# A two-layer decoder trunk on one core: the block gather between two engines' layouts done as 16 SBUF copies instead of a trip through DRAM

## The chip, the cores and the metric

The kernel runs on one core of one Trainium2 chip. Its time is the device time of one launch in microseconds (us); less is better. The engines named here: PE (TensorE, matrix products and transposes), ACT (ScalarE), DVE (VectorE), POOL (GpSimd) and SP (SyncE, which only issues transfers here). Each engine works through its own instruction list in order, and instructions wait for one another by semaphores. SBUF is the on-chip memory with 128 partitions, PSUM the accumulators that PE writes, DRAM the large memory outside the core.

## The reference

A trunk of two layers on 256 positions of width 2048, all in float32. Cut to what is computed:

```python
for l in range(2):
    h = rms_norm(x, mix_norm[l])
    q, k, v, uv, gate_logits = split(h @ w_in[l])                  # 2048 x 7680
    q = rope(rms_norm(q, q_norm[l])); k = rope(rms_norm(k, k_norm[l]))
    a = sliding_window_attention(q, k, v, sinks[l]) @ w_attn_branch[l]   # 16 heads of 64, 4 kv heads
    b = chunked_sgu(gelu(uv), w_spatial[l], ...) @ w_sgu_branch[l]
    g = sigmoid(gate_logits)
    x = x + (g[:, :2048] * a + g[:, 2048:] * b) @ w_out[l]
    h2 = rms_norm(x, ffn_norm[l])
    x = x + (silu(h2 @ w_gate[l]) * (h2 @ w_up[l])) @ w_down[l]    # inner width 5632
```

## The kernel before, in words

**The products.** Every large product is a weight matrix (read once from DRAM) times activations of 256 positions. A float32 product is made of three reduced-precision ones: weights and activations are both split into a high part (`whi`, `uh`) and the rest (`wlo`, `ul`), and PE adds whi x uh, wlo x uh and whi x ul (lines 287 to 289). For that, a piece of weights of 256 x 512 arrives in `raw`, ACT copies it to `whi` (line 201), and DVE subtracts to get `wlo` (line 202). `raw` has 5 buffers and `whi` and `wlo` have 4 each, so the `whi` of one piece can't be written before PE is done with the piece four earlier.

**The stream.** All pieces of both layers stand in one list of 1010 entries, in PE's order (class `Stream`). At each entry the program asks for the raw piece 7 ahead (W_LOAD), the split 4 ahead (W_SPLIT) and sums of weights 6 ahead (W_SUM). A plain entry (X, G or U) has 12 matmuls of 128 x 512. The pairs of products `mix` (w_out), `ffn` (gate and up) and `hid` (down) use the Strassen-Winograd scheme for their first unit of activations: its entries P1 to P7 have 6 matmuls each, need sums of weights (line 189, DVE) and sums of activations (line 439, DVE, then split into `sh` and `sl` at lines 430 and 431), and copies of intermediate results, `snap` (line 313, ACT). The entries P1, P2, P6, P7 and P4 of a pair are woven between the last four entries of the plan before it; P6 accumulates on P1's result and so waits for P1's snap. The feed-forward part is done in three rounds per layer, of 4, 4 and 3 pairs `ffn`, each followed by two pairs `hid`.

**Activations as PE needs them.** PE wants the activations with the contracted dimension across partitions, so each 256 x 512 block of x, q, k, gate, hid and so on is transposed into a unit. Mostly that is done by `turn`: DVE transposes 32 x 32 blocks into `box` (line 355), and then the blocks have to move across partitions, the gather (lines 359 to 363). Before the change SP writes the box to a DRAM tile `far` (512 KB) and reads it back in four transfers into `tt` (128 KB each). ACT and DVE then scale and split `tt` into `uh` and `ul` (lines 381 to 390), or for Winograd units into `flat`, sums, `sh` and `sl`. For a few last units that are needed at once, PE transposes instead (`pt`, line 399).

**What sets the order.** PE's order is the program's own. The program counts ticks: one for about 12 matmuls of the stream; `after(n, f)` calls `f` n ticks later, and that is where turns, readers of turns and norms are put. The order of the other engines' lists is then made by a scheduler from a model of the timeline, with the ticks as the earliest place. `box` has one buffer.

Of the kernel before, what the change touches and what calls it, by code (L numbers as in the profile page):

```python
# [8 lines left out]
F32 = mybir.dt.float32  # L9
# [5 lines left out]
P = 128  # L15
NT = 2
# [17 lines left out]
WINO = 0  # L34
TAIL = 2
W_SPLIT = 4
W_SUM = 6
N_WARM = 8
TT = 1
# [12 lines left out]
def hybrid_trunk(ctx: ExitStack, tc: tile.TileContext, x, mix_norm, w_in, q_norm, k_norm, sinks,  # L52
# [9 lines left out]
    tmp = ctx.enter_context(tc.tile_pool(name="tmp", bufs=5))  # L62
    dram = ctx.enter_context(tc.tile_pool(name="dram", bufs=2, space=bass.MemoryType.DRAM))
    turned = ctx.enter_context(tc.tile_pool(name="turned", bufs=TT))
# [53 lines left out]

    def pair(key, wa, wb, late=False):
# [15 lines left out]
        body = [g[0], p5, g[1], p3] + g[2:-2] + u[:-TAIL] + g[-2:] + u[-TAIL:] if late else \  # L135
            [g[0], p5, g[1], p3] + g[2:] + u
        return Plan(key, head, body)

    plans = []
    for l in range(DEPTH):  # L140
        wl = w_in[l]
        for kind, c in FIRST_PART:
            o = {"kv": O_KV, "q": 0, "v": O_V, "u": O_U, "gate": O_GATE}[kind] + c * CW
            plans.append(single(("in", l), wl[:, o:o + CW]))
        plans += [single(("att", l), w) for w in cols_of(w_attn_branch[l], NCH)]
        for j in range(NCH):
            plans.append(single(("in", l), wl[:, O_GATE + D + j * CW:O_GATE + D + (j + 1) * CW]))
            plans.append(single(("sgu", l), w_sgu_branch[l, :, j * CW:(j + 1) * CW]))
        c_ = cols_of(w_out[l], NCH)
        plans += [pair(("mix", l), c_[j], c_[j + 1]) for j in range(0, NCH, 2)]  # L150
        for r, (f0, f1) in enumerate(ROUNDS):
            for f in range(f0, f1):
                plans.append(pair(("ffn", l), w_gate[l, :, f * CW:(f + 1) * CW], w_up[l, :, f * CW:(f + 1) * CW]))
            c_ = cols_of(w_down[l, f0 * CW:f1 * CW, :], NCH)
            plans += [pair(("hid", l, r), c_[j], c_[j + 1], j == 0) for j in range(0, NCH, 2)]
# [8 lines left out]
    class Stream:  # L164
# [41 lines left out]
        def next(self):  # L206
            self.load(self.at + W_LOAD)
            self.split(self.at + W_SPLIT)
            self.add(self.at + W_SUM)
            self.at += 1  # L210
            return self.parts[self.at - 1]
# [136 lines left out]
    def turn(dst, src):  # L348
# [7 lines left out]

        far = dram.tile([P, 4, 4 * NT * B], F32, tag="far", name=nm("far"))

        def gather():
            nc.sync.dma_start(far, box.rearrange("p j k t r -> p j (k t r)"))  # L360
            for j in range(4):
                nc.sync.dma_start(dst[j * B:(j + 1) * B].rearrange("c i k t r -> c i (k t r)"),
                                  far[:, j].rearrange("(i c) x -> c i x", c=B))

# [3 lines left out]
    def transposed(units, c, src, cols=None, on_pe=False, wino=False):  # L368
# [41 lines left out]
        if not wino:  # L410
# [3 lines left out]

            after(5, lambda: parts(0, 2, blocks_of(0)))
            after(6, done)
            return
# [28 lines left out]

        after(5, lambda: scaled(0))
        after(6, lambda: scaled(2))
        after(7, sums)
        after(8, finished)  # L450

# [36 lines left out]
    norm.unit(0, True)  # L488
    stream.split(W_SPLIT)
    after(1, lambda: norm.unit(1, True))  # L490
# [107 lines left out]
    class Attention:  # L598
# [65 lines left out]
        def turn_queries(self, c, q):  # L664
# [6 lines left out]
            turn(tt, q)  # L671
            after(4, lambda: ordered(0))
            after(5, lambda: ordered(2))

# [129 lines left out]
    def residual(key, nxt=None, scale=1.0, store=False):  # L804

        def chunk(j, sums):
# [11 lines left out]
            if nxt is not None:  # L818
                after(2, lambda: nxt.unit(j, j == NCH - 1))
                after(3, lambda: nxt.squares(j))  # L820
# [9 lines left out]
    for l in range(DEPTH):  # L830
# [31 lines left out]
        for j in range(NCH):  # L862
            gb = gate(l)
            ps = product(("sgu", l))
            for t in range(NT):
                nc.vector.scalar_tensor_tensor(out=gb[:, t, :], in0=gb[:, t, :], scalar=1.0, in1=ps[t],
                                               op0=ALU.add, op1=ALU.mult)
                nc.vector.tensor_tensor(out=ga[j][:, t, :], in0=ga[j][:, t, :], in1=gb[:, t, :], op=ALU.add)
            after(2, lambda j=j: transposed(mT, j, ga[j], on_pe=j == NCH - 1, wino=j == WINO))
            tick()  # L870
# [7 lines left out]
        def hidden(hT, c):  # L878
# [15 lines left out]
            def on_up(sums):  # L894
                up = added(sums)
                for t in range(NT):
                    nc.vector.scalar_tensor_tensor(out=hid[:, t, :], in0=up[t], scalar=norm.rr[t], in1=hid[:, t, :],  # L897
                                                   op0=ALU.mult, op1=ALU.mult)
                after(2, lambda: transposed(hT, c, hid, on_pe=c == len(hT) - 1 == 2, wino=c == WINO))

# [51 lines left out]
```

## Time and profile before

| | us |
|---|---|
| time, median of 3 runs (lowest to highest) | 2535.17 (2532.13 to 2540.45) |
| the profiled execution: its own time | 2530.42 |
| its span, first to last instruction | 2528.7 |
| PE busy | 2480.7 (98%) |
| DVE busy | 1906.9 (75%) |
| ACT busy | 1334.7 (53%) |
| POOL busy | 43.8 (2%) |

The mean granted clock of PE was 0.994 of full speed. The page has, per group of instructions, the line, the engine, the operation and the tiles (out<-in), then the busy time, the mean time of one in ns, and the engine's idle time just before them with what ended most of it. The view of waits lists, for one engine, who it waited for: the total in us, the number of times and the longest. The timeline has the start and the length in us; in brackets stands the idle time before and its releaser. Rows of stretches (A:B) list the length and, for PE, weight load, DVE, ACT and POOL, the busy time, then the granted clock, the share of the DMA engines and GB/s. An engine name with q is its queue of transfers.

### The profile page before, as it was taken

What the parts mean: (1) busy time and instruction counts of PE and PEld (TensorE: products, weight loads), DVE (VectorE), ACT (ScalarE), POOL (GpSimd) and SP (SyncE); (2) the same over time, 40 slices, a digit from 0 to 9 for tenths busy, and PEclk for the clock granted to TensorE, in tenths of its full rate; (3) what the DMA queues carried; (4) which work ended last, traced back from release to release, by engine and by line L of the source; (5) the groups of instructions that cost most, each with busy time, mean ns of one, the idle gap of its engine ahead of it and who ended that gap; (6) DMA issues with size and microseconds to landing.
All of it is one profiled execution on the core that took longest, in us unless ns stands there. A gap on an engine that the chain in (4) does not pass through costs nothing.

```text
span 2528.7 us, 30348 instructions
## 1 busy us (share of the span) xinstructions
PE 2480.7 (98%) x11094; PEld 2043.9 (81%) x11094; DVE 1906.9 (75%) x2293; ACT 1334.7 (53%) x1658; POOL 43.8 (2%) x47
## 2 busy tenths in 40 slices
PE   8999999999999999999999999999999999999999
PEld 7888888878788878887778888887778888788877
DVE  6786556787878787868877865568888777877787
ACT  5555444565555555555555554446555555555554
POOL 1100000000000000000000000000000000000000
PEclk9999999999999999999999999999999999999999
DMA  8755667676666667665776556666756666676654
GB/s 274 249 157 174 218 214 229 201 237 198 208 233 202 214 203 230 203 214 189 226 238 221 178 172 208 225 214 201 233 186 219 218 216 193 213 236 199 218 188 146
DMA packets 284823, 530.77 MB, mean 210 GB/s; under 512 B 18880, under 2 KB 46624, under 8 KB 284672
## 3 DMA queue, kind: packets, MB, share of 16 engines
q1 hardware_dynamic: 284000, 528.29, 64.5%
q8 instruction: 87, 1.43, 0.2%
q0 software_dynamic: 352, 0.25, 0.1%
q14 instruction: 64, 0.52, 0.1%
q10 hardware_dynamic: 320, 0.27, 0.0%
HBM read 500.96 MB, written 27.79 MB: 209 GB/s over the span
## 4 chain that ended last, share of the span: by engine, by line
PE 91%; DVE 3%; DMA 3%; ACT 2%; issue 1%; SPq 0%; DVEq 0%; ACTq 0%
PE acc L287 29%; PE acc L289 29%; PE acc L288 29%; DVE wlo L202 2%; ACT whi L201 1%; PE po L723 1%; DMA far<-box 1%; DMA raw<-in_w_in_dram 1%; PE psc L684 1%; PE ppt L713 0%; DMA raw<-in_w_gate_dram 0%; DVE raw L189 0%; DMA tt<-far 0%; PE pt L399 0%; DVE xs L813 0%
## 5 line engine op out<-in xcount | busy, mean ns | idle before, releaser
L202 DVE TENSOR_TENSOR wlo<-raw,whi 128x1024 fp32r<-128x1024 f32 (+1 forms) x1012 | 1227.7, 1220 | 506.9 <-ACT whi L201 487.6
L201 ACT ACTIVATE whi<-raw 128x1024 fp32r<-128x1024 f32 (+1 forms) x1012 | 1059.9, 1056 | 924.2 <-PE acc L289 682.6
L287 PE MATMUL acc<-whi,uh 128*128 128x512 f32 x3204 | 1257.2, 392 | 0.8 <-ACT uh L385 0.5
L289 PE MATMUL acc<-whi,ul 128*128 128x512 f32 x3204 | 1250.1, 390 | 3.9 <-DVE ul L390 3.9
L288 PE MATMUL acc<-wlo,uh 128*128 128x512 f32 x3204 | 1251.1, 390 | 2.7 <-DVE wlo L202 2.7
L289 PEld LDWEIGHTS acc<-whi,ul 128*128 128x128 f32 x3204 | 603.6, 188 | 131.4 <-DVE ul L390 4.8
L288 PEld LDWEIGHTS acc<-wlo,uh 128*128 128x128 f32 x3204 | 603.8, 188 | 130.6 <-DVE wlo L202 6.2
L287 PEld LDWEIGHTS acc<-whi,uh 128*128 128x128 f32 x3204 | 603.7, 188 | 127.4 <-ACT snap L313 1.5
L189 DVE TENSOR_TENSOR raw<-raw,raw 128x1024 f32<-128x1024 f32 x152 | 185.5, 1220 | 1.0
L287 PE MATMUL acc<-whi,sh 128*128 128x512 f32 x304 | 121.2, 399 | 26.4 <-ACT snap L313 26.4
L289 PE MATMUL acc<-whi,sl 128*128 128x512 f32 x304 | 120.1, 395 | 0.0
L288 PE MATMUL acc<-wlo,sh 128*128 128x512 f32 x304 | 120.0, 395 | 0.0
L287 PEld LDWEIGHTS acc<-whi,sh 128*128 128x128 f32 x304 | 57.7, 190 | 41.4 <-ACT snap L313 29.8
L313 ACT ACTIVATE snap<-acc 128x512 f32<-128x512 f32 x114 | 67.8, 594 | 37.9 <-PE acc L289 37.9
L381 ACT ACTIVATE uh<-tt 128x512 fp32r<-128x512 f32 x52 | 30.1, 624 | 77.4 <-DMA tt<-far 77.4
L289 PEld LDWEIGHTS acc<-whi,sl 128*128 128x128 f32 x304 | 58.1, 191 | 12.4
L288 PEld LDWEIGHTS acc<-wlo,sh 128*128 128x128 f32 x304 | 58.1, 191 | 11.7
L382 DVE TENSOR_TENSOR ul<-tt,uh 128x512 fp32r<-128x512 f32 x52 | 35.8, 688 | 36.9 <-ACT uh L381 36.9
L813 DVE SCALAR_TENSOR_TENSOR xs<-acc,xs 128x512 f32<-128x512 f32 (+1 forms) x66 | 42.7, 668 | 9.2 <-PE acc L289 9.2
L884 DVE TENSOR_TENSOR snap<-acc,snap 128x512 f32<-128x512 f32 x66 | 45.3, 687 | 5.4 <-PE acc L289 5.3
L813 DVE SCALAR_TENSOR_TENSOR xs<-snap,xs 128x512 f32<-128x512 f32 (+1 forms) x50 | 33.0, 663 | 0.0
L897 DVE SCALAR_TENSOR_TENSOR hid<-snap,rr,hid 128x512 f32<-128x512 f32 x44 | 32.6, 741 | 0.0
(132 smaller groups left out, 831.5 us busy)
## 6 DMA issues: line engine op xcount, KB each, us to landing
raw<-in_w_in_dram SPq DMA_DIRECT2D x239, 512.0 KB, 4.2
raw<-in_w_up_dram SPq DMA_DIRECT2D x176, 512.0 KB, 4.9
raw<-in_w_gate_dram SPq DMA_DIRECT2D x176, 512.0 KB, 4.2
raw<-in_w_down_dram SPq DMA_DIRECT2D x176, 512.0 KB, 4.6
raw<-in_w_out_dram SPq DMA_DIRECT2D x64, 512.0 KB, 4.7
far<-box SPq DMA_DIRECT2D x49, 512.0 KB, 6.0
tt<-far SPq DMA_DIRECT2D x188, 128.0 KB, 3.4
raw<-in_w_attn_branch_dram SPq DMA_DIRECT2D x32, 512.0 KB, 4.3
```

The source lines that it names most:

```text
L189: self.last = nc.vector.tensor_tensor(out=self.raws[d], in0=self.raws[x], in1=self.raws[y], op=ALU.add if op == "+" else ALU.subtract)
L201: nc.scalar.activation(hi[:, i, :], raw[:, i, :], AF.Copy)
L202: self.last = nc.vector.tensor_tensor(out=lo[:, i, :], in0=raw[:, i, :], in1=hi[:, i, :].bitcast(F32), op=ALU.subtract)
L287: nc.tensor.matmul(ps, a, hi[:, kk, :], start=first and kk == 0, stop=False, skip_group_check=True)
L288: nc.tensor.matmul(ps, a, lo[:, kk, :], start=False, stop=False, skip_group_check=True)
L289: nc.tensor.matmul(ps, b, hi[:, kk, :], start=False, stop=kk == 1, skip_group_check=True)
L313: nc.scalar.activation(p.snaps[tag], a[1], AF.Copy)
L381: nc.scalar.activation(h, s_, AF.Copy)
L382: nc.vector.tensor_tensor(out=l, in0=s_, in1=h.bitcast(F32), op=ALU.subtract)
L813: nc.vector.scalar_tensor_tensor(out=xs[:, t, sl], in0=part[:, i * w:(i + 1) * w], scalar=scale, in1=xs[:, t, sl], op0=ALU.mult, op1=ALU.add)
L884: nc.vector.tensor_tensor(out=x[1], in0=x[0], in1=x[1], op=ALU.add)
L897: nc.vector.scalar_tensor_tensor(out=hid[:, t, :], in0=up[t], scalar=norm.rr[t], in1=hid[:, t, :], op0=ALU.mult, op1=ALU.mult)
```

## The change

Six edits. (1) The gather becomes 16 copies from SBUF to SBUF, one for each pair of a source and a target group of 32 partitions (32 x 1 KB each), all issued from POOL's queue; the DRAM tiles are gone. (2) Everything that reads a turned block is put one tick later (6 and 7 instead of 5 and 6; for Winograd units 6 to 9 instead of 5 to 8; for queries 5 and 6 instead of 4 and 5). (3) The first pair `ffn` of each layer and the first pair `hid` of each round take their later entries unit by unit: after the first entries G and U alternate in twos. Before, all G stood ahead of all U, and the first pair of each round's `hid` had its last two G just ahead of the last two U. (4) For the first 10 entries the split is 3 ahead instead of 4 (W_FIRST). (5) At the boundary between the layers the last but one norm unit is also transposed on PE, so there are 48 turns instead of 49. (6) The transposes on PE of the last units of mix, hid and norm are put one tick later (3 instead of 2).

```diff
-        far = dram.tile([P, 4, 4 * NT * B], F32, tag="far", name=nm("far"))
-
         def gather():
-            nc.sync.dma_start(far, box.rearrange("p j k t r -> p j (k t r)"))
             for j in range(4):
-                nc.sync.dma_start(dst[j * B:(j + 1) * B].rearrange("c i k t r -> c i (k t r)"),
-                                  far[:, j].rearrange("(i c) x -> c i x", c=B))
+                for i in range(4):
+                    nc.gpsimd.dma_start(dst[j * B:(j + 1) * B, i], box[i * B:(i + 1) * B, j])
...
-            after(5, lambda: parts(0, 2, blocks_of(0)))
-            after(6, done)
+            after(6, lambda: parts(0, 2, blocks_of(0)))
+            after(7, done)
...
-        after(5, lambda: scaled(0))
-        after(6, lambda: scaled(2))
-        after(7, sums)
-        after(8, finished)
+        after(6, lambda: scaled(0))
+        after(7, lambda: scaled(2))
+        after(8, sums)
+        after(9, finished)
...
-            after(4, lambda: ordered(0))
-            after(5, lambda: ordered(2))
+            after(5, lambda: ordered(0))
+            after(6, lambda: ordered(2))
...
-        body = [g[0], p5, g[1], p3] + g[2:-2] + u[:-TAIL] + g[-2:] + u[-TAIL:] if late else \
-            [g[0], p5, g[1], p3] + g[2:] + u
+        body = [g[0], p5, g[1], p3] + g[2:] + u
+        if by_unit:
+            body = [g[0], p5, g[1], p3] + u[:2]
+            for i in range(2, len(rest), 2):
+                body += g[i:i + 2] + u[i:i + 2]
...
-                plans.append(pair(("ffn", l), w_gate[l, :, f * CW:(f + 1) * CW], w_up[l, :, f * CW:(f + 1) * CW]))
+                plans.append(pair(("ffn", l), w_gate[l, :, f * CW:(f + 1) * CW], w_up[l, :, f * CW:(f + 1) * CW], f == 0))
...
-            self.split(self.at + W_SPLIT)
+            self.split(self.at + (W_FIRST if self.at < N_FIRST else W_SPLIT))
...
-                after(2, lambda: nxt.unit(j, j == NCH - 1))
+                after(3 if j == NCH - 1 else 2, lambda: nxt.unit(j, j == NCH - 1 or j == NCH - 2 and not nxt.wino))
...
-            after(2, lambda j=j: transposed(mT, j, ga[j], on_pe=j == NCH - 1, wino=j == WINO))
+            after(2 + (j == NCH - 1), lambda j=j: transposed(mT, j, ga[j], on_pe=j == NCH - 1, wino=j == WINO))
...
-                after(2, lambda: transposed(hT, c, hid, on_pe=c == len(hT) - 1 == 2, wino=c == WINO))
+                pe = c == len(hT) - 1 == 2
+                after(3 if pe else 2, lambda: transposed(hT, c, hid, on_pe=pe, wino=c == WINO))
```

What the scheduler makes of it is seen in the engines' lists, at three places. (Line numbers of the changed kernel are up to two higher or one lower; the number behind a tile's name counts tiles and tells pieces apart.) First, DVE in layer 0, where the first block of queries, q0, is rotated and transposed into its box. Before, from the piece of entry 24 on:

```order
L202 TENSOR_TENSOR wlo_137_774<-raw_125_712,whi_136_773 128x1024
L640 TENSOR_TENSOR q_110_657<-q_110_657,sq_111_660 128x1024
L202 TENSOR_TENSOR wlo_143_796<-raw_128_731,whi_142_795 128x1024
L355 STREAM_TRANSPOSE box_139_790<-q_110_657 128x4x4x32 x2
L202 TENSOR_TENSOR wlo_146_820<-raw_131_750,whi_145_819 128x1024
L202 TENSOR_TENSOR wlo_155_850<-raw_135_771,whi_154_849 128x1024
```

and with the change:

```order
L204 TENSOR_TENSOR wlo_141_803<-raw_127_739,whi_140_802 128x1024
L622 TENSOR_TENSOR q_109_665<-q_109_665,rq_111_669 128x1024
L628 TENSOR_TENSOR sq_110_668<-q_109_665,sa0_0_400 128x16x32 x2
L204 TENSOR_TENSOR wlo_144_838<-raw_130_758,whi_143_837 128x1024
L633 TENSOR_TENSOR q_109_665<-q_109_665,ca0_0_399 128x1024
L204 TENSOR_TENSOR wlo_153_868<-raw_134_779,whi_152_867 128x1024
L639 TENSOR_TENSOR q_109_665<-q_109_665,sq_110_668 128x1024
L204 TENSOR_TENSOR wlo_159_892<-raw_139_800,whi_158_891 128x1024
L357 STREAM_TRANSPOSE box_138_798<-q_109_665 128x4x4x32 x2
```

Before, the two transposes follow the `wlo` of entry 25 (the second `wlo` shown); now they follow that of entry 28 (the fourth).

Second, ACT at the same place: the reader of q0's turned block is `qT`, and the scores of attention on PE, which need it, stand in both programs between entries 28 and 29. Before, from the `whi` of entry 25 on (`sq` is the square of the second block of queries):

```order
L201 ACTIVATE whi_142_795<-raw_128_731 128x1024
L201 ACTIVATE whi_145_819<-raw_131_750 128x1024
L201 ACTIVATE whi_154_849<-raw_135_771 128x1024
L201 ACTIVATE whi_160_873<-raw_141_793 128x1024
L616 ACTIVATE sq_148_838<-q_147_835 128x1024
L201 ACTIVATE whi_163_894<-raw_144_817 128x1024
L668 ACTIVATE qT_113_662<-tt_138_789 128x512 x2
L201 ACTIVATE whi_166_914<-raw_153_847 128x1024
```

and with the change, from the same entry on:

```order
L203 ACTIVATE whi_140_802<-raw_127_739 128x1024
L203 ACTIVATE whi_143_837<-raw_130_758 128x1024
L203 ACTIVATE whi_152_867<-raw_134_779 128x1024
L203 ACTIVATE whi_158_891<-raw_139_800 128x1024
L203 ACTIVATE whi_161_911<-raw_142_835 128x1024
L203 ACTIVATE whi_164_931<-raw_151_865 128x1024
L615 ACTIVATE sq_146_856<-q_145_853 128x1024
L203 ACTIVATE whi_167_951<-raw_157_889 128x1024
L203 ACTIVATE whi_178_993<-raw_160_909 128x1024
L667 ACTIVATE qT_112_670<-tt_137_797 128x512 x2
L203 ACTIVATE whi_183_1014<-raw_163_929 128x1024
```

The reader `qT` stood behind the `whi` of entry 29; now it stands behind that of entry 32.

Third, ACT at the head of the third pair `ffn` of layer 0, from the `whi` of its P2 (entry 226) to the snap of P1. Before:

```order
L201 ACTIVATE whi_1050_5259<-raw_1037_5185 128x1024
L201 ACTIVATE whi_1052_5277<-raw_1041_5207 128x1024
L201 ACTIVATE whi_1055_5318<-raw_1032_5162 128x1024
L201 ACTIVATE whi_1060_5332<-raw_1049_5257 128x1024
L201 ACTIVATE whi_1063_5344<-raw_1033_5164 128x1024
L430 ACTIVATE sh_1047_5253<-sums_1044_5232 128x1024
L201 ACTIVATE whi_1065_5361<-raw_1054_5316 128x1024
L313 ACTIVATE snap_1059_5330<-acc_1058_5323 128x512
```

and with the change:

```order
L203 ACTIVATE whi_1038_5415<-raw_1027_5343 128x1024
L429 ACTIVATE uh_997_5192<-flat_1026_5340 128x1024
L203 ACTIVATE whi_1041_5456<-raw_1018_5300 128x1024
L203 ACTIVATE whi_1046_5470<-raw_1033_5391 128x1024
L203 ACTIVATE whi_1049_5482<-raw_1019_5302 128x1024
L203 ACTIVATE whi_1051_5499<-raw_1040_5454 128x1024
L429 ACTIVATE sh_1036_5411<-sums_1032_5386 128x1024
L315 ACTIVATE snap_1045_5468<-acc_1044_5461 128x512
```

The last `whi` ahead of the snap is that of entry 231 in both. Before, `sh` stands ahead of that `whi`; now it stands behind it, directly ahead of the snap, and `uh` has moved in behind the `whi` of entry 227.

On POOL the gather of q0 is one row of 16, with the power function `rq` of the first queries and two triangular cuts of the spatial weights ahead of it and `rq` of the second queries behind it:

```order
L263 TENSOR_TENSOR rq_111_669<-ssq_114_673,neg_half_132 128x16
L549 AFFINE_SELECT wsraw_133_776<-wsraw_133_776 128x512
L549 AFFINE_SELECT wsraw_156_885<-wsraw_156_885 128x512
L362 DMA tt_137_797<-box_138_798 32x256 x16
L263 TENSOR_TENSOR rq_147_857<-ssq_150_861,neg_half_132 128x16
L362 DMA tt_180_1009<-box_181_1010 32x256 x16
```

Before, the same stretch of POOL's list was the two `rq` with the two cuts between them.

More of the change, by code (lines that the diff above doesn't have):

```diff
@@ L34 @@
 WINO = 0
-TAIL = 2
 W_SPLIT = 4
 W_SUM = 6
+W_FIRST, N_FIRST = 3, 10
 N_WARM = 8
@@ L62, in hybrid_trunk @@
     tmp = ctx.enter_context(tc.tile_pool(name="tmp", bufs=5))
-    dram = ctx.enter_context(tc.tile_pool(name="dram", bufs=2, space=bass.MemoryType.DRAM))
     turned = ctx.enter_context(tc.tile_pool(name="turned", bufs=TT))
@@ L117, in single, with pair @@
         return Plan(key, [], [half(w, h, "X") for h in range(w.shape[0] // (2 * P))])
-    def pair(key, wa, wb, late=False):
+    def pair(key, wa, wb, by_unit=False):
         h1, h2 = 2 * WINO, 2 * WINO + 1
@@ L488, in hybrid_trunk @@
     norm.unit(0, True)
-    stream.split(W_SPLIT)
+    stream.split(W_FIRST)
     after(1, lambda: norm.unit(1, True))
```

## The prediction

> **What bounds the kernel now.** I read the page first, for the busiest engine.
>
> ```profile
> span 2528.7 us, 30348 instructions
> PE 2480.7 (98%) x11094; PEld 2043.9 (81%) x11094; DVE 1906.9 (75%) x2293; ACT 1334.7 (53%) x1658; POOL 43.8 (2%) x47
> L201 ACT ACTIVATE whi<-raw 128x1024 fp32r<-128x1024 f32 (+1 forms) x1012 | 1059.9, 1056 | 924.2 <-PE acc L289 682.6
> L313 ACT ACTIVATE snap<-acc 128x512 f32<-128x512 f32 x114 | 67.8, 594 | 37.9 <-PE acc L289 37.9
> ```
>
> TensorE works 2480.7 of 2528.7 us, so this change, which takes away no matmul of the products, can only win from some 48 us of idle PE and from matmuls at a lower clock, and it loses wherever PE waits anew. The view of what PE waited for says where the idle time is (total, times, longest):
>
> ```profile
> PE acc L287 <- ACT snap L313: 26.7, 9, 4.5
> PE pt L399 <- DVE xs L813: 4.5, 3, 2.8
> PE acc L289 <- DVE ul L390: 3.9, 2, 3.4
> PE pt L399 <- DVE hid L897: 2.6, 2, 2.0
> PE pt L399 <- DVE gate L868: 2.0, 1, 2.0
> ```
>
> No row names a transfer: PE never waits directly for the way through DRAM. The largest wait is for `snap`, the copy of P1's result. Six of its nine waits are long, at the heads of the ffn pairs 2, 6 and 10 of each layer. One of them, in the timeline:
>
> ```profile
> 1145.92 1.22 DVE L189 TENSOR_TENSOR raw<-raw,raw 128x1024 f32<-128x1024 f32 x1
> 1147.26 2.95 ACT L201 ACTIVATE whi<-raw 128x1024 fp32r<-128x1024 f32 x3 [5.53 <-DVE raw L189]
> 1150.12 1.04 ACT L430 ACTIVATE sh<-sums 128x1024 fp32r<-128x1024 f32 x1
> 1151.06 1.04 ACT L201 ACTIVATE whi<-raw 128x1024 fp32r<-128x1024 f32 x1
> 1152.01 0.57 ACT L313 ACTIVATE snap<-acc 128x512 f32<-128x512 f32 x1
> 1152.64 0.75 PE L287 MATMUL acc<-whi,sh 128*128 128x512 f32 x1 [3.78 <-ACT snap L313]
> ```
>
> ACT sat idle 5.53 us for DVE's weight sum, then did four `whi` and one `sh` before the `snap`: ACT's queue is in order and the snap stands last. Now the stretches of four us right after each of the six, and the sum of six stretches of 8 to 8.5 us that end at them (busy PE, and PEclk near the row's end):
>
> ```profile
> 636.50:640.50 4.00, 3.94 (x11) 3.10 (x12) 2.69 (x4) 1.54 (x3) 0.00 (x0) 0.60 0.71 242
> 894.70:898.70 4.00, 3.90 (x17) 3.25 (x18) 3.35 (x4) 1.59 (x3) 0.00 (x0) 1.00 0.67 227
> 1152.60:1156.60 4.00, 3.96 (x10) 3.14 (x11) 2.65 (x3) 1.05 (x2) 0.00 (x0) 0.57 0.66 222
> 1894.20:1898.20 4.00, 3.97 (x9) 3.14 (x10) 2.65 (x3) 1.00 (x2) 0.00 (x0) 0.50 0.73 248
> 2154.70:2158.70 4.00, 3.96 (x12) 3.21 (x13) 3.32 (x4) 1.54 (x2) 0.00 (x0) 0.69 0.73 237
> 2413.30:2417.30 4.00, 3.94 (x9) 3.14 (x10) 2.68 (x3) 0.98 (x3) 0.00 (x0) 0.50 0.70 232
> 886.70:894.70 8.00, 4.71 (x21) 3.57 (x19) 7.13 (x8) 5.28 (x6) 0.00 (x0) 1.00 0.28 87
> sum 48.50, PE 25.85 PEld 18.50 DVE 44.09 ACT 31.14 POOL 0.00; mean PE 4.31 PEld 3.08 DVE 7.35 ACT 5.19 POOL 0.00
> ```
>
> The six stalls cost 48.5 - 25.85 = 22.65 us of idle PE, and five of them a second time: the clock granted afterwards is 0.50 to 0.69, so (1 - clock) x 4 us makes 1.6 + 0 + 1.7 + 2.0 + 1.2 + 2.0 = 8.5 us. The one at 894.7, with 8.00 - 4.71 = 3.3 us idle, the shortest, kept its clock. The Trainium skill, "TensorE: Matmul & The Clock Gate", Part 1, says that an idle window of some 3.4 us halves the clock; the trace agrees. So about 31 us hang on these six places.
>
> **The change, part by part.** The sum goes against the profiled execution, 2530.42 us; the median of the runs shown, 2535.17, is 4.75 us higher, and I add that at the end.
>
> *The way through DRAM.* Going: 49 writes and 196 reads on SP's queue. Their direct worth to PE is 0 by the waits above; ACT's waits for `tt` are covered by the `whi` that stand four entries ahead. Without that cover each late `tt` would cost what q0 costs below. New: 16 transfers in a row on POOL's queue per turn, and in the program built, each waits for the landing of the one eight before it. Their price isn't in the trace; the nearest rows are these (landing: median us from issue; the DMA rows of POOL with their issue time):
>
> ```profile
> cs<-in_cosine_dram POOLq DMA_DIRECT2D x1, 32.0 KB, 5.0
> gn<-in_k_norm_dram POOLq DMA_DIRECT2D x2, 32.0 KB, 7.3
> kT<-far SPq DMA_DIRECT2D x8, 128.0 KB, 3.0
> out_dram<-xs SPq DMA_DIRECT2D x6, 256.0 KB, 2.2
> 40.71 1.23 DVE L202 TENSOR_TENSOR wlo<-raw,whi 128x1024 fp32r<-128x1024 f32 x1
> 41.10 0.53 POOL L257 DMA_DIRECT2D gn<-in_q_norm_dram  x1 [34.23 <-DVE sa L574]
> ```
>
> An issue takes 0.53 us, also while DVE works on a `wlo`. With a landing of L, a gather takes max(8 x 0.53, L) + 7 x 0.53 + L: 10.2 us for L = 2.2, 18.6 for 7.3. I take L = 4.1, between the 3.0 of kT (the same bytes landing in SBUF) and the 5.0 of POOL's own 32 KB: 12.1 us. Readers now come one tick, about 2.7 us, later, and in the order most of them stand 7 to 9 `whi` behind their box, so 19 us or more: hidden.
>
> *q0, the exception.* Before:
>
> ```profile
> 81.12 1.29 DVE L355 STREAM_TRANSPOSE box<-q 128x512 f32<-128x512 f32 x2
> 87.66 1.39 DVE L202 TENSOR_TENSOR wlo<-raw,whi 128x1024 fp32r<-128x1024 f32 x1 [0.17 <-ACT whi L201]
> 92.86 1.15 ACT L668 ACTIVATE qT<-tt 128x512 f32<-128x512 f32 x2 [2.46 <-DMA tt<-far]
> 97.02 0.39 PE L289 MATMUL acc<-whi,ul 128*128 128x512 f32 x1
> 97.34 0.72 PE L684 MATMUL psc<-kT,qT 64*128 64x128 f32 x8
> 97.44 1.06 ACT L201 ACTIVATE whi<-raw 128x1024 fp32r<-128x1024 f32 x1 [1.54 <-PE acc L289]
> ```
>
> The box was done at 82.4; the scores started 0.3 us after the last product ahead of them, with no wait. By the orders, the box moves from behind the `wlo` of entry 25 to behind that of entry 28 (the one at 87.66, done 89.05), so to 90.3, and qT from behind the `whi` of entry 29 to behind that of entry 32 (the one at 97.44). The scores stay where they are. So they wait for 90.3 + 12.1 + 0.6 (half of qT) = 103.0 instead of 97.3: 5.7 us, and by the rows above a stall of this length costs 1.6 us of clock as well: 7.3. POOL's `rq` of q1 stands behind the 16 issues, till 98 or so, and DVE's step that needs it stands ahead of later `wlo`; and the one box has to be read out before q1's transposes, now 9 to 12 us behind. Both waits end by 103 and so lie beside PE's own: nothing more is charged. The same place returns in layer 1: 14.6 us for both. Bounds: L = 2.2 gives 3.8 each, 7.6; L = 7.3 gives 12.2 + 1.7, about 28.
>
> *The six snaps.* The chain of sums on DVE that holds ACT up loses the `ul`, the small `sums` and a `wlo` that stood ahead of the second weight sum, so ACT should no longer be late there. But in ACT's new order the `whi` of entry 231 now stands ahead of `sh`, and both ahead of the snap. That `whi` needs the buffer of the entry that PE just finished, so PE still waits 1.06 + 1.04 + 0.59 = 2.7 us, if DVE is in time with `sums`. Bounds: 0 (as now) to -14.7 (six at 2.7, the clock loss partly kept). I take 3.3 us each, the length that kept its clock: 19.8 for 22.65, and two thirds of the 8.5: -8.6.
>
> *New and moved forced waits of the same kind* (something PE needs next stands behind a `whi` that needs PE's last entry). Prices from this row, with `whi` and `snap` above:
>
> ```profile
> 1265.71 1.71 ACT L385 ACTIVATE uh<-tt,vcols 128x256 fp32r<-128x256 f32 x4 [5.15 <-DMA tt<-far]
> 1271.42 0.33 PE L399 MATMUL pt<-ident,xs 128*128 128x128 f32 x1 [2.84 <-DVE xs L813]
> ```
>
> The first head of ffn in each layer: 1.06 + 1.71 + 0.59 = 3.4 us, twice, against about 4 us (26.7 - 22.65) that the two and a shorter one cost now: +3. The last G of the first hid pair in rounds 0 and 1 of layer 0, which by_unit leaves nearer to the turned third unit: 1.06 and half of an `uh` pair, about 2 each: +4. First pair of mix in layer 1, P1 behind a tanh: +1.7. The layer boundary trades its wait of 2.8 us on the transposes (row 1271.42) for 1.06 + 1.71 behind a `whi`: 0.
>
> *Transposes on PE a tick later*: the three waits on `hid` and `gate` (2.6 + 2.0) have a tick of 2.7 us more and go, and 1.4 of the rest: -6. *W_FIRST = 3* puts one split less ahead of the first norm units, whose `ul` PE waited for 3.9: -2.5 (bounds 0 and -3.9).
>
> Sum: -8.6 - 6 - 2.5 + 14.6 + 3 + 4 + 1.7 = +6.2, on 2530.4 makes 2536.6, as a median of runs 2541. That is 0.2% above before.
>
> **A page that speaks against it.** The Trainium skill, "SBUF — State Buffer", the "DVE blocks DMA" trap, says that descriptors of a GpSimd DMA can't be written while DVE runs in a mode that takes the shared port, and advises a queue of ACT or SP. By the row at 41.10 an issue under a running `wlo` was not held.
>
> **Rivals.**
> - *A, the forecast*: gather hidden but for q0. 2541.
> - *B, faster*: landings of 2.2 us and DVE in time everywhere. q0 costs 7.6, the snaps bring -14.7, the first units -3.9: -14.7 - 6 - 3.9 + 7.6 + 8.7 = -8.3, so 2527. For it: DRAM traffic of half a MB each way per turn goes, SP no longer sits behind a write, and ACT's idle 5.53 us came from DVE, whose order got shorter. Against: the snap stays behind a `whi` that PE itself releases.
> - *C, slower*: the two groups of eight each pay a long landing. From L = 7.3 on a gather takes 18.6 us, q0 costs 28, and the hid and xs units with 19 us to spare begin to hold ACT's queue, `whi` and then PE: some ten of the 48 by 1 us each. +6.2 + 13.4 + 10 = +30, so 2565; at L = 5.5, where only q0 grows, 2550. For it: POOL's landings of 5.0 and 7.3. Against: they came from DRAM in the busy start.
> - *D, the port*: each of 16 issues is held by a DVE operation of 1.2 us for up to that time. A gather then takes 16 x 1.75 + 4 = 32 us, past the reader of nearly every turn by 10: with PE's cover of some 8 us, 2 us on 48 turns and 20 more on each q0: +130. Against: the issue of 0.53 at 41.10. The trap of "SBUF — State Buffer" would do this for some DVE operations.
>
> **How the numbers follow.** A measurement here tells 0.3%, 7.6 us, from no change: 2527.6 to 2542.8. Chances: A 0.55, B 0.22, C 0.19, D 0.04. A's own range, with q0 at 7.6 or at 18 (L = 5.5) and each other term at half or one and a half, is 2531 to 2551; it falls into "same" 6 times in 10 and above it 3; B lies at the lower bound, more often below it; C and D are slower. Faster: 0.55 x 0.1 + 0.22 x 0.75 = 0.22, with a little for gains that no wait shows, 0.25; slower: 0.55 x 0.3 + 0.23 = 0.38; same 0.37. The range goes from below B's 2527 to C's milder price: 2523 to 2560.
>
> **What would show it.** In the changed profile: PE waiting for qT near 97 and 1350 us by 4 to 12 us with a clock below 1 after it (q0); POOL's 16 issues at 0.53 apart, eight and eight, with a gap if L is over 4.2; snap waits of about 2.7 to 3.3 at the six places and windows at clock 1.00 behind them; waits on `uh` in the first hid pairs; no wait of `pt` for `hid`. I am wrong if PE waits for `tt` or its readers in many turns (C or D), if the snap waits vanish, or if q0 shows none.

## The result, and the profile after

The changed kernel is 1.3% slower: median 2566.31 us (2562.82 to 2568.65, 4 runs) against 2533.65 us; the ratio is 1.013 with a 95% interval of 1.0096 to 1.0164. The forecast was 2541 with a range of 2523 to 2560, so the time lies above the range. The profiled execution of the changed kernel took 2568.65 us. Its page, with the total, the row of the copies on POOL, and the row of the DMA issues (the median landing stands last):

```profile
span 2566.9 us, 31129 instructions
PE 2496.1 (97%) x11102; PEld 2055.7 (80%) x11102; DVE 1912.0 (74%) x2291; ACT 1341.9 (52%) x1658; POOL 420.4 (16%) x815
L362 POOL DMA_DIRECT2D tt<-box x736 | 362.1, 499 | 1753.5 <-DVE box L357 561.3
tt<-box POOLq DMA_DIRECT2D x736, 32.0 KB, 4.3
```

One copy takes POOL 0.499 us to issue and lands after 4.3 us: the two prices that the trace of before didn't hold (0.53 and 4.1 were taken) were nearly right. What PE waited for, in the changed kernel:

```profile
PE acc L289 <- ACT snap L315: 35.1, 8, 7.7
PE psc L683 <- ACT qT L667: 14.1, 2, 7.1
PE acc L291 <- DVE ul L381: 4.8, 4, 1.4
PE acc L289 <- ACT uh L380: 3.3, 2, 1.7
PE acc L291 <- DVE ul L389: 2.6, 1, 2.6
PE acc L289 <- ACT gate L799: 1.8, 1, 1.8
```

The waits for `pt` (9.1 us before) are gone; the snap's grew from 26.7 to 35.1, and qT, `uh` and `ul` of turned units are new. The clock fell too. The view of the cores, of the changed kernel:

```profile
core 0: 2566.9 us, clock 0.986
```

It was 0.994 before. What that cost shows in PE's busy time, since the products are the same: it grew from 2480.7 to 2496.1 us. So some 15 of the 38 us between the spans are matmuls that ran slowly behind a wait, and the other 23 are the waits themselves (PE idle for 48.0 us before and 70.8 after). In the records of the granted clock of both traces every low stretch up to the last matmul, at 0.50, lasts 3.4 or 6.8 us, and stalls of one length can go with either: before the change, two waits of 3.79 us (at 1894 and 2155 us) went with 6.8 and with 3.4 us.

Where the 38 us lie can be told entry by entry, since PE's stream has 1010 entries in both. The difference of the times at which the same entry starts in the two traces grows or falls at a few places only:

| place (entries) | forecast | measured |
|---|---|---|
| q0, scores behind qT (29 and 534) | +14.6 | +9.7 and +9.3 |
| snaps of ffn pairs 2, 6, 10 (six places) | -8.6 | +4.6 |
| first hid pairs, turned units (281, 395; 786, 900) | +4 | +12.9; +2.8 |
| first head of ffn (190, 695) | +3 | +4.8 |
| first pair of mix, layer 1 (654) | +1.7 | +2.0 |
| boundary between layers (502 to 509) | 0 | +2.2 |
| PE's transposes (480, 662, 700) | -6 | -7.4 |
| second pair of mix, layer 0 (175 to 179) | - | -1.1 |
| start | -2.5 | -1.9 |
| elsewhere, in small steps | - | +0.4 |
| sum | +6.2 | +38 |

Most places were named with the right sign; the sizes were not right, and one sign, that of the six snaps, was wrong. Of the 32 us between the two sums, 13.2 lie at the snaps, 11.7 at the turned units of the first hid pairs and 4.4 at q0. First q0, from the timeline of the changed kernel (POOL's rows from the timeline of POOL alone; `kT` are the turned keys, gathered just before q0):

```profile
67.23 1.48 POOL L362 DMA_DIRECT2D kT<-box  x3 [2.18 <-DMA kT<-box]
68.72 2.93 POOL L263 TENSOR_TENSOR rq<-ssq,neg_half 128x16 f32<-128x16 f32 x1
87.30 1.29 DVE L357 STREAM_TRANSPOSE box<-q 128x512 f32<-128x512 f32 x2
88.88 4.47 POOL L362 DMA_DIRECT2D tt<-box  x9 [3.72 <-DVE box L357]
93.84 0.50 POOL L362 DMA_DIRECT2D tt<-box  x1 [0.49 <-DMA tt<-box]
95.44 0.50 POOL L362 DMA_DIRECT2D tt<-box  x1 [1.10 <-DMA tt<-box]
96.23 2.45 POOL L362 DMA_DIRECT2D tt<-box  x5 [0.29 <-issue]
101.90 1.15 ACT L667 ACTIVATE qT<-tt 128x512 f32<-128x512 f32 x2 [5.28 <-DMA tt<-box]
102.58 1.62 PE L683 MATMUL psc<-kT,qT 64*128 64x128 f32 x8 [7.11 <-ACT qT L667]
```

The box was done at 88.6 (90.3 was forecast) and the last copy landed 13.2 us later: copies of the second eight wait for landings of the first, one by one. Over all 48 turns the time from the box's end to the last landing has a median of 13.9 us (10.9 to 16.6); through DRAM it was 11.0 (7.3 to 17.8). The new way is the longer one. PE waited 7.1 us, and the scores and the next product then ran at a granted clock of 0.54 to 0.56.

Why the box is late can be read from the first two rows. POOL computes `rq`, the power function that q0's rotation needs, and in its list `rq` stands behind the 16 copies of the keys. Its input was ready at 63.8 us, but it started only at 68.7, when the last copy had been issued, and ended at 71.7; DVE's list has the first step that uses it later still, at 78.7. Before, `rq` started 0.1 us behind its input (68.5) and was used at 72.5. So POOL's own work is held up by the row of copies too, and in DVE's list the steps that need it have moved back further than that.

At the other places `tt` had long landed. The view of ACT's waits has only qT waiting for it (10.5 us, twice); the other readers start 15 to 27 us behind their box (median 18.0; before, 7 to 18, median 11.3), because they stand behind splits in ACT's list. The head of the third ffn pair, changed kernel:

```profile
641.49 3.49 DVE L204 TENSOR_TENSOR wlo<-raw,whi 128x1024 fp32r<-128x1024 f32 x3
641.90 1.06 ACT L203 ACTIVATE whi<-raw 128x1024 fp32r<-128x1024 f32 x1 [1.66 <-PE acc L291]
644.89 1.22 DVE L191 TENSOR_TENSOR raw<-raw,raw 128x1024 f32<-128x1024 f32 x1
646.03 0.42 DVE L438 TENSOR_TENSOR sums<-sums,flat 128x256 f32<-128x256 f32 x1
646.36 1.22 DVE L204 TENSOR_TENSOR wlo<-raw,whi 128x1024 fp32r<-128x1024 f32 x1
647.50 0.42 DVE L438 TENSOR_TENSOR sums<-flat,sums 128x256 f32<-128x256 f32 x1
647.95 1.06 ACT L429 ACTIVATE sh<-sums 128x1024 fp32r<-128x1024 f32 x1 [5.00 <-DVE sums L438]
648.91 0.58 ACT L315 ACTIVATE snap<-acc 128x512 f32<-128x512 f32 x1
649.55 0.79 PE L289 MATMUL acc<-whi,sh 128*128 128x512 f32 x1 [7.68 <-ACT snap L315]
```

ACT was through with the last split at 643.0 and could have taken the snap then. But `sh`, which belongs to a unit of the hid pairs, stands ahead of it, and the sums that this `sh` needs are finished at 647.9. Before, ACT was late at this place (by a weight sum); now it stands idle for 5.0 us in front of work that P6 doesn't need. The extra tick is not what makes the sums late: with the old ticks (below) ACT waits 5.1 us for them at the same place. This is the longest of the six waits. They are 7.7, 4.7 and 4.7 us in layer 0 (4.5, 3.4 and 3.8 before) and 4.1, 3.7 and 3.7 in layer 1 (3.8, 3.8 and 3.7 before), and at the other five places ACT stood 1.0 to 2.1 us for the sums. And the last turned unit of the first hid pair:

```profile
770.27 1.06 ACT L203 ACTIVATE whi<-raw 128x1024 fp32r<-128x1024 f32 x1 [1.66 <-PE acc L291]
771.24 1.14 ACT L380 ACTIVATE uh<-tt 128x512 fp32r<-128x512 f32 x2
771.90 0.50 PE L289 MATMUL acc<-whi,uh 128*128 128x512 f32 x1 [1.67 <-ACT uh L380]
773.32 1.29 DVE L381 TENSOR_TENSOR ul<-tt,uh 128x512 fp32r<-128x512 f32 x2
774.06 0.79 PE L291 MATMUL acc<-whi,ul 128*128 128x512 f32 x1 [1.42 <-DVE ul L381]
```

with the stretches around it and, last, behind the snap above:

```profile
771.00:774.00 3.00, 0.73 (x2) 0.30 (x2) 2.97 (x5) 1.37 (x3) 0.00 (x0) 0.88 0.00 0
774.00:778.00 4.00, 3.94 (x9) 3.14 (x10) 0.61 (x2) 0.00 (x0) 0.00 (x0) 0.50 0.46 135
649.50:653.50 4.00, 3.95 (x9) 3.14 (x10) 0.77 (x1) 0.99 (x2) 0.00 (x0) 0.50 0.29 107
```

PE waits twice, 1.67 us for `uh` and 1.42 us for the `ul` that is computed from it, and has two matmuls between. For the next four us the clock is 0.50. At the same place in layer 1 there was one wait, of 0.97 us for `ul` (at 2054.6), and the clock behind it stayed at 1.00.

### The profile page after: what moved, and what is told of

Same layout as the page of the kernel before. It is cut to its first block, busy times and chain, and to the rows that moved or that the text cites. A ratio compares the mean times of both kernels' runs of the same rounds, so it can differ in the third digit from the quotient of the medians.

```text
span 2566.9 us, 31129 instructions
## 1 busy us (share of the span) xinstructions
PE 2496.1 (97%) x11102; PEld 2055.7 (80%) x11102; DVE 1912.0 (74%) x2291; ACT 1341.9 (52%) x1658; POOL 420.4 (16%) x815
## 5 line engine op out<-in xcount | busy, mean ns | idle before, releaser
L362 POOL DMA_DIRECT2D tt<-box x736 | 362.1, 499 | 1753.5 <-DVE box L357 561.3
L289 PE MATMUL acc<-whi,sh 128*128 128x512 f32 x304 | 122.3, 402 | 35.1 <-ACT snap L315 35.1
L687 DVE TENSOR_TENSOR pr<-psc,mask 128x256 f32<-128x256 f32 (+1 forms) x32 | 17.3, 552 | 23.1 <-PE psc L683 23.1
```

Source lines behind the costliest of these rows:

```text
L289: nc.tensor.matmul(ps, a, hi[:, kk, :], start=first and kk == 0, stop=False, skip_group_check=True)
L362: nc.gpsimd.dma_start(dst[j * B:(j + 1) * B, i], box[i * B:(i + 1) * B, j])
L687: nc.vector.tensor_tensor(out=pr[:, :, j, :nk], in0=pscore[:, :, :nk], in1=mk.unsqueeze(1).to_broadcast([P, 2, nk]), op=ALU.add)
```

## The experiments

Four theories are told apart. O: the loss comes from the place of readers in ACT's and DVE's lists, behind splits that wait for PE. T: it comes from the readers' later ticks and the entries unit by unit. R and L: it comes from the real time of the copies, R as the longer gather, L as a length that no place in the list can hide. All runs are compared with the kernel before on the same chip, in the same rounds; ratios have their 95% interval.

**The route alone, taken back.** The changed kernel with the gather through DRAM:

```diff
...
+            nc.sync.dma_start(far, box.rearrange("p j k t r -> p j (k t r)"))
             for j in range(4):
-                for i in range(4):
-                    nc.gpsimd.dma_start(dst[j * B:(j + 1) * B, i], box[i * B:(i + 1) * B, j])
+                nc.sync.dma_start(dst[j * B:(j + 1) * B].rearrange("c i k t r -> c i (k t r)"),
+                                  far[:, j].rearrange("(i c) x -> c i x", c=B))
```

> The changed kernel with the gather through DRAM as before; everything else of the change stays. Theory O (order): the 38 us come from where ACT's and DVE's lists put the readers of the turned blocks, behind splits that wait for PE; with the DRAM route the list has qT behind the split of entry 29 again, and no reader of a hid unit behind a split of entry 284 or 398. So the 19 us at q0, the 13 + 2.5 at the hid units, the 5 at the layer boundary go, the gains on PE's transposes (8.5) and at the start (2) stay, the six snap waits stay about as in the changed kernel (+5): 2528, within 2520 to 2536. Theory T (ticks and entry order): what costs is that readers are put a tick later and pairs go unit by unit; then it stays above 2555.

Measured: 2519.85 us, ratio 0.9945 (0.9929 to 0.9961), 8 us better than O's number and just below its range; theory T, which had it above 2555, is out. So the route costs 46 us, and the rest of the change wins 13. In its waits no qT and no unit of a hid pair is left; the snaps are:

```profile
PE acc L290 <- ACT snap L316: 25.2, 8, 4.2
```

They cost about what they did before (26.7), not more, although the readers and the sums are a tick later here too.

**The route alone, done.** The kernel before with nothing changed but the 16 copies on POOL's queue.

> The kernel before with only the gather changed to 16 copies from POOL's queue; ticks, entry order and all else as before. O: the list has the same readers behind the same splits as the changed kernel (qT behind the split of 32, hid units behind those of 284 and 398, and at 786 and 900 too), without the gains of the small edits: 2534 + 38 + 10 = 2580, within 2565 to 2592. T: near before, 2527 to 2541.

Measured: 2603.82 us, ratio 1.0282 (1.0267 to 1.0298), 71 us slower and 12 above O's range; T had it near the kernel before. The same places answer as in the changed kernel, and more of them. Its PE waits:

```profile
PE acc L286 <- ACT snap L312: 37.8, 8, 5.9
PE psc L680 <- ACT qT L664: 13.3, 2, 7.0
PE acc L288 <- DVE ul L386: 6.9, 3, 3.6
PE acc L286 <- ACT uh L381: 6.8, 3, 4.3
PE acc L286 <- ACT uh L377: 6.7, 4, 1.7
```

Without the other edits the layer boundary alone, where two turned norm units come late, adds 9 us, and all four hid units cost 5 to 6.5 us.

**The ticks taken back.** The changed kernel with its readers at the old ticks (5 and 6, queries 4 and 5, Winograd units 5 to 8).

```diff
-            after(6, lambda: parts(0, 2, blocks_of(0)))
-            after(7, done)
+            after(5, lambda: parts(0, 2, blocks_of(0)))
+            after(6, done)
```

> The changed kernel (16 copies from POOL) with the readers' ticks as before the change. The prediction had put qT's new place behind the split of entry 32, and the hid units' places, down to readers that come one tick later. If that were so, the 19 us at q0 and the 15.5 us at the hid units go: 2535 or less. If the scheduler puts them there because it counts the 16 transfers from POOL as long (its list has the same places without the tick), nothing is gained: 2560 to 2578.

Measured: 2587.52 us, ratio 1.0222 (1.02 to 1.0245): 21 us slower than the changed kernel, outside the range given on the far side. The later tick isn't what moved the readers; qT stands behind the split of entry 32 and the hid units behind those of 284 and 398 in this list as well, and the two of layer 1, which the tick had put one split earlier, too. The lists fit a scheduler that places readers by the time at which it counts the copies as landed; how it counts is not in the record, only the lists are. So the extra tick of the change was a help against its own new route.

**The 16 copies from another queue.** The changed kernel with `nc.sync` in place of `nc.gpsimd`.

> The changed kernel with the same 16 copies issued from SP's queue instead of POOL's. O: the list has no reader behind a split that PE waits on, except the six snaps: 2520 to 2535. If the copies between partitions themselves were the cost (theory R, the real length of the gather), it stays at 2555 or more; if SP's queue is held up by 16 issues of some 0.4 us, raw loads come late and it lies between.

Measured: 2532.76 us, ratio 0.9995 (0.9986 to 1.0004). The forced waits are gone from the list, and the time is within O's range, but the gain of the small edits is eaten. The DMA row of this run:

```profile
tt<-box SPq DMA_DIRECT2D x736, 32.0 KB, 1.9
```

A copy issued here lands after 1.9 us instead of 4.3, but one issue took SP 0.59 us (median); 16 of them hold the queue that loads all weights for about 10 us, and PE then waits 8.2 us in 17 waits for `wlo` (1.3 with the DRAM route) and 29.9 us for snaps (25.2). The box-to-landing median is 11.7 us. So a row of 16 on one queue need not cost 46 us; the row on POOL's queue does.

**The place in the list, without the length.** The changed kernel with its readers pinned: a split written behind a reader is also queued behind it on ACT. The readers of units that PE transposes are pinned in the same way. The edit at the split (the readers' lines, which set `kept`, are left out):

```diff
-                    nc.scalar.activation(hi[:, i, :], raw[:, i, :], AF.Copy)
+                    with ExitStack() as pinned:
+                        if self.kept is not None:
+                            pinned.enter_context(tc.issue_after(self.kept.ins))
+                        nc.scalar.activation(hi[:, i, :], raw[:, i, :], AF.Copy)
...
```

> The changed kernel, copies from POOL's queue as they are, with one thing more: a split that the program writes behind a reader of a turned block is also queued behind it on ACT, so that the readers keep their place in the program. O: the waits at the hid units (15.5 us) and the boundary (5) go, q0 is down to what the landing of 13.2 us costs behind its late box (4 us each instead of 9.5), the six snap waits stay: 2538, within 2530 to 2546. R (the copies' real length of 14 instead of 11 us is what costs): it stays within 6 us of 2566.

Measured: 2574.41 us, ratio 1.0164 (1.0147 to 1.0181). The expectation of theory O failed. The waits at the two hid units went (6.5 us each) and q0 gave back 2.4 each time, but more than that came back elsewhere. ACT's row for the turned units, first before the change and then in this run:

```profile
ACT uh L381 <- DMA tt<-far: 77.4, 22, 5.8
ACT uh L384 <- DMA tt<-box: 80.7, 19, 9.6
```

and what PE waited for in this run:

```profile
PE acc L293 <- ACT snap L319: 30.9, 8, 5.5
PE acc L294 <- DVE wlo L208: 11.9, 22, 0.9
PE acc L293 <- ACT whi L207: 11.2, 7, 2.4
```

With the reader in its place in the program, ACT reaches it before the copies have landed (14.3 us in the median) and stands still, with the next splits queued behind it. The total of such waits is no larger than before the change, when PE felt none of them, but single ones are longer: 12 over 5 us, against 4. Three of PE's seven waits for `whi` (5.3 of the 11.2 us) come within 2 us of such a landing. Two others (3.8 us, at entries 176 and 700) don't: there the reader itself stands behind ACT's wait for `xs` from DVE, with the splits pinned behind both, and PE's stream loses 4.8 us at each place. So some 10 us of this run come with the pin and not with a landing, and it doesn't decide between O and R. The same pin with another route was not run.

**The same a tick later.** Pinned readers, all ticks one more (7 and 8, and so on), so that they come behind the landing.

> As the run with pinned readers (POOL copies, splits written behind a reader also queued behind it), with every reader of a turned block one more tick later (7 and 8, queries 6 and 7, Winograd units 7 to 10). The readers then stand some 16 us behind the box, behind the measured landing of 14.3, and in the list none of them stands behind a split that PE waits on. Theory O (the place in the list costs, not the length of the copy): ACT no longer waits for landings, the waits at hid units and boundary stay away, q0 keeps 4 to 5 us each, the six snaps stay: 2538, within 2528 to 2548. Theory L (with 14 us a copy is too long for any place; only its length matters): it stays within 8 us of 2566 to 2574.

Measured: 2547.48 us, ratio 1.0056 (1.0041 to 1.0071): just inside O's range, at its upper end, 19 us below the changed kernel and 28 above the DRAM route. So the place in the list carries part of the loss. What else it carries stays open, since two places in the lists are still bad: in layer 0 the snaps stand behind `sh` (7.3, 4.2 and 4.2 us of the 25.1 that PE waits for snaps), and the box of q0 still comes behind the split of entry 28. The copies of q0 landed after 10.4 us in both layers, no later than through DRAM (10.3 and 11.3), and 8.6 us of waits for qT are left all the same: at q0 it is the late box more than the copy. ACT also still waits for some landings (23.4 us in six waits for turned units).

**Two queues.** The changed kernel with the copies dealt out, eight from POOL and eight from SP.

```diff
-                    nc.gpsimd.dma_start(dst[j * B:(j + 1) * B, i], box[i * B:(i + 1) * B, j])
+                    eng = nc.gpsimd if i % 2 else nc.sync
+                    eng.dma_start(dst[j * B:(j + 1) * B, i], box[i * B:(i + 1) * B, j])
```

> The changed kernel with the 16 copies dealt to two queues, eight from POOL and eight from SP. Eight issues of 0.5 us and a landing of 4.3 make some 8.5 us from box to landing instead of 13.9, and SP is held for some 5 us per turn instead of 10. The list has no reader behind a split that PE waits on, except the snaps. Both O and L: the 46 us that the POOL route costs against DRAM go, 2520, within 2512 to 2530. If SP's 8 issues cost as half of what 16 did (about 13 us between the run with SP copies and the one with DRAM), 2526.

Measured: 2503.2 us, ratio 0.988 (0.9866 to 0.9895): 63 us below the changed kernel and 17 below DRAM, better than the range given (2512 to 2530). A turn in its timeline:

```profile
1838.68 0.70 DVE L357 STREAM_TRANSPOSE box<-hid 128x512 f32<-128x512 f32 x1
1839.41 5.25 SPq L363 DMA_DIRECT2D tt<-box  x8
1840.22 3.98 POOL L363 DMA_DIRECT2D tt<-box  x8 [36.62 <-issue]
1854.50 1.33 ACT L426 ACTIVATE flat<-tt 128x256 f32<-128x256 f32 x4
```

No copy waits for the landing of another any more; from box to landing it takes 8.2 us in the median. POOL now issues only eight copies of the keys ahead of `rq`, q0's box comes at entry 25 again, and none of the waits for qT or for turned units of hid pairs is left.

**Two queues alone.** The kernel before with only that.

> The kernel before with only the gather changed, to 16 copies dealt to POOL's and SP's queues; the twin of run x3_gather (all 16 on POOL, 2604). If it is the length of one queue's row of 16 that costs, from box to landing 14 us against 8, this is some 75 us faster than x3_gather and a little faster than before: 2527, within 2515 to 2537. If copies between partitions cost by themselves (their share of the DMA engines, or POOL's issues beside DVE), at least half of the 71 us stays: 2565 or more.

Measured: 2508.43 us, ratio 0.9907 (0.9889 to 0.9926): 95 us below its twin with all copies on POOL, and below the range given (2515 to 2537). The same 16 copies, between the same partitions, win 23 us or lose 71, by whether POOL's queue has all of them or half.

**The small edits alone.** The kernel before with the first splits 3 ahead, PE's transposes a tick later and the extra norm unit on PE.

> The kernel before with only the small edits: split 3 ahead for the first 10 entries, the last but one norm unit on PE at the layer boundary, PE's transposes a tick later. Gather through DRAM, readers' ticks and order of entries as before. By the places in run x1_dram: start -4, transposes -9, boundary -3: 2532 - 14 = 2518, within 2512 to 2525; then the readers' tick and by_unit together are worth nothing beside x1_dram's 2520. If they are the gain, it stays above 2526.

Measured: 2521.27 us, ratio 0.9957 (0.994 to 0.9974), inside the range given and, as far as can be told, the 2519.85 of the DRAM run. The later readers and the entries unit by unit together are worth nothing with the DRAM route.

**The snap pinned.** The kernel before, and the changed kernel with the DRAM route, with a split that is written behind a snap also queued behind it (the edit at the split is the one shown above).

```diff
-            nc.scalar.activation(p.snaps[tag], a[1], AF.Copy)
+            stream.kept = nc.scalar.activation(p.snaps[tag], a[1], AF.Copy)
```

> The kernel before with one edit: a split that the program writes behind a snap is also queued behind it on ACT, so that P1's snap no longer stands behind four splits and sh. If the place of the snap is what made the six long waits (22.65 us idle and 8.5 us of low clock), P6 then waits only for its own split weights, under 1 us: 2532 - 28 = 2504, within 2497 to 2512. If DVE's late weight sums are what holds these places, the wait only changes its name (from snap to whi or wlo of P6) and less than 10 us are gained.

> The changed kernel with the gather through DRAM as before (run x1_dram, 2520) and the snaps pinned as in the run on the kernel before. Both gains are at different places and should add: 25.2 us of snap waits and some 8 of clock go: 2490, within 2483 to 2502; better than both kernels.

Measured: 2522.91 us, ratio 0.9947 (0.9927 to 0.9966), on the kernel before, and 2499.0 us, ratio 0.9861 (0.9847 to 0.9876), on the other. On the first only 11 of 28 us came; the second is within the range given. PE's waits in the first:

```profile
PE acc L292 <- DVE wlo L206: 9.7, 19, 1.3
PE acc L291 <- ACT snap L317: 9.3, 9, 2.1
PE pt L403 <- DVE xs L817: 5.6, 2, 4.2
```

The long snap waits went (17 us less), but 7 us came back as waits for `wlo` (2.7 before) and 1 at PE's transposes, and the mean clock rose only from 0.994 to 0.995. On the other kernel the pin is worth 21 us: there too `wlo` costs more (7.5 us for 1.3), but no wait is longer than 2.5 us and the mean clock is 1.000.

**The best of both.** Two queues and pinned snaps, in the changed kernel.

> The changed kernel with the copies dealt to POOL's and SP's queue (run b2_mix, 2503) and the snaps pinned (which took 21 us off the DRAM version). Left in b2_mix are 20.2 us of snap waits and some 8 us of low clock behind them; the pin leaves a wait for wlo there. 2503 - 18 = 2485, within 2478 to 2493. If the two routes only differ by what the snaps cost them, it ends near the 2499 of the DRAM version with pins.

Measured: 2480.35 us, ratio 0.9798 (0.9777 to 0.9819), within the range given and the fastest here: 51 us below the kernel before, 86 below the changed one. What PE still waits for:

```profile
PE acc L293 <- ACT snap L319: 4.1, 4, 1.4
PE acc L294 <- DVE wlo L208: 3.1, 9, 0.6
```

## Why the prediction was wrong, point by point

- *What bounds the kernel* held: PE waits for engines' work, never directly for a transfer, and the change could only work through what stands in ACT's and DVE's lists.
- *The price of a gather* held for its parts (0.50 and 4.3 us for 0.53 and 4.1), less for the whole: 13.9 us for 12.1, since the landings of the first eight are spread and the second eight wait for them one at a time. (Two small slips: by its own formula the bound for L = 7.3 is 18.3 us and not 18.6, and the snaps' term is -8.5. Neither matters.) That this is longer than the old way's 11.0 was in the trace of before, but the two were never put side by side; "hidden, 19 us or more" looked only at the distance to the readers.
- *Readers stand 7 to 9 splits behind, so hidden* is the step that failed. Being landed in time isn't enough. A reader that far back in ACT's list is itself late: readers start 15 to 27 us behind their box instead of 7 to 18, and the units' users on PE did not move. It was put down to the extra tick; the run with the old ticks has the same places and is 21 us slower. The cause is the row of 16 copies on POOL's queue: with the DRAM route, with all copies on SP, or with eight each on POOL and SP, the readers that PE waited for are back within three splits of their old places. In what shares this row costs by the way the scheduler counts it and by its real length, the two runs with pinned readers (2574 and 2547) don't settle.
- *q0*: right mechanism, 19.0 us for 14.6. Against the trace of before, the box came 6.2 us later in time (88.6 for 82.4), 8.1 against PE's stream, which was 1.9 us ahead there; the copies took 2.9 us longer (13.2 for 10.3). So about three quarters are the late box. That it came late was read from the orders; why it did, `rq` behind the copies of the keys, was not seen. The landing came 1.1 us later than taken (12.1), and the stall with the clock behind it was 9.7 and 9.3 us for 7.3.
- *The six snaps*: wrong sign, +4.6 for -8.6, the largest miss. ACT was no longer late, as said, but "if DVE is in time with `sums`" was the condition, and it was not met: `sh` stood waiting at all six, 12.5 us in all and 5.0 at the worst. In layer 1 the waits (4.1, 3.7, 3.7) are near the 3.3 taken, in layer 0 (7.7, 4.7, 4.7) they are not, and the clock behind all six fell to 0.50 to 0.58 where two thirds of that loss were to go. The bound "0, as now" was no bound; nothing held it there.
- *The hid units*: right places, 15.7 us for 4. The second wait, for `ul`, was left out, and no loss of clock was charged behind waits this short. The two layer 1 units were left out altogether.
- *Transposes on PE, start, first heads, mix*: within 2 us each. The layer boundary, put at 0, took 2.2.
- *The rivals*: none is what happened. C's 2565 is near the time by luck, since its mechanism isn't there: a landing takes 4.3 us and not 7.3, and readers other than qT waited for no landing. D is ruled out: 736 issues had a mean of 0.499 us with DVE busy for 74% of the time.
- *The median*: the 4.75 us added for the difference between the profiled run and the median weren't there after; the profiled run of the changed kernel lies 2.3 us above its median.

What stays open is how the 46 us of the route divide between the length that the scheduler counted and the real one; every edit of the route changed both, and the pins brought waits of their own. The runs show that the place of the readers carries at least the 19 us that pinning them late gave back. Whether the rest is the list as well (the late box, the snaps of layer 0) or the real length is not shown.

## What to carry to other kernels

When a transfer gets a new route, compare box-to-landing times first, and then read in each engine's list what stands ahead of the reader: a reader that waits behind work released by its own consumer is late however early its data lands. A row of small transfers in one queue that waits for its own landings should be dealt to two queues before it is judged. And look at what else the issuing engine has to compute: it stands behind the row. An instruction that PE needs next, like the snap, is worth pinning ahead of work that only needs to be done soon.

## What the runs showed of the hardware that was not expected

Two waits of 1.67 and 1.42 us, with 0.7 us of matmuls in the three us around them, were followed by four us at a clock of 0.50; a single stall of 3.3 us before the change had left the clock at 1.00. The same 32 KB copy within SBUF landed after 4.3 us (median) when POOL issued it and after 1.9 us when SP issued all 16; dealt to both, it was 4.3 us on either.
